# All of w_down in MLP groups 0 to 5 by seven products, with the 1/rms scale moved to the addition to the residual

## The chip, the cores and the metric

The kernel runs on one core of a Trainium2 chip. The metric is the device time of one execution in microseconds (us), the median of several runs. The engines are TensorE (PE in the profile, its weight loads PEld), VectorE (DVE), ScalarE (ACT), GpSimd (POOL) and SyncE (SP, which here only issues transfers).

## The reference

Two layers over 256 tokens of width 2048, all in float32. Each layer is a block of three attention groups and then an MLP; the change touches the MLP:

```python
h = rmsnorm(x, norm_mlp[l])
u = relu(h @ w_up[l])          # (256, 2048) @ (2048, 8192)
x = x + (u * u) @ w_down[l]    # (256, 8192) @ (8192, 2048)
```

`rmsnorm` multiplies a token's row by r = 1/sqrt(mean(x^2) + eps) and a column by its gain. Since r is positive and one number a token, relu(r a)^2 = r^2 relu(a)^2.

## The kernel before

Precision: a weight tile of float32 is split into a rounded part `hi` (format fp32r) and the rest `lo`; activations likewise. Three products (hi hi, lo hi, hi lo) stand for one float32 product. The split of a tile of 128 x 1024 (512 KB) is one cast on ACT (L1036) and one subtraction on DVE (L1037). `whi` and `wlo` have three buffers each, the raw tiles `wraw` five, `side` four, `spare0` and `spare1` one each.

The program is a list of `Step`s, one weight tile each. The main loop at the end of `tile_trunk` goes through it: it issues loads up to seven steps ahead on SP (`LOOK_LOAD`), splits two or three ahead, calls a step's `prep` five to eight ahead (`LOOK_PREP`, `LOOK_T2`, `LOOK_T3`), and then emits the step's matmuls. Tile's scheduler turns that into a fixed order for each engine, and may move an instruction past others that wait. `tick()` emits pieces of background work (the `add` queue) by their costs and due times.

The MLP is cut into eight groups `g` of 1024 columns of w_up, each of four blocks `q` of 256:

- `up_steps`: four steps a block, each with eight matmuls of 512 columns (L675: hi weights times hi and lo activations) and eight of 256 (L680: lo weights). At the fourth, `evac` copies the two banks out (L653 ACT, L654 DVE), takes the relu and multiplies by r (L655, one DVE instruction against `rrow`, r written along a row for all partitions), squares (ACT), splits into `u` (L660, L661), and `sums_of` makes the four sums S1 to S4 of the seven-product scheme from it (`sT`). `rrow` is built once a layer by `rows`: r on a diagonal, two fp32 matmuls with ones (L505), a copy.
- `strassen_steps(g, pair)`: Winograd's form of Strassen's scheme. A is u^2 of the group, its two token blocks times its blocks' two column halves; B is w_down, two halves along the sum times two blocks of 512 output columns. `pair` 0 is output columns 0 to 1023, `pair` 1 is 1024 to 2047. The sum of 1024 goes in two tiles, h = 0 and 1. The products in order are P1 = A11 B11, P2 = A12 B21, P7 = S3 (B12+B22), P6 = S2 (B22+B11+B12), P5 = S1 (B11+B12), P3 = S4 B22, P4 = A22 (B22+B11+B12+B21): each one step of six matmuls (L806) a tile. Bank `a` takes P1, P6, P5, P3, bank `d` takes P7 and P4; both lie in the one tile `S`. Bank `b` takes P2. After its product a bank is added to or subtracted from the residual `x` on DVE (L777) and, in `a` and `d`, accumulated on.
- Sums of weights come in two ways. `on_top` is a transfer from POOL that adds a tile from memory to one in SBUF (L792): on B11 for P2's step, on B12 for P7's, on P6's sum for P4. `sum_of` is a DVE addition (L788): P6's.
- `down_steps`: plain steps of twelve matmuls (L468, in `mode_b`), then an addition to `x` (L728).

In groups 0 to 5 the second half of the columns is mixed: its tile h = 0 goes by seven products (seven steps), its tile h = 1 plain, in four steps. Two of these (columns 1536 to 2047) have banks of their own; the two for columns 1024 to 1535 come at the end of the group and accumulate on banks `b` and `d` of the products. Groups 6 and 7 have seven products for the first half and plain steps for the second. While group g's down steps run, the up steps of group g + 1 are laid between them by a list `order` (1: a seven-product step, 0: another):

```python
for p_ in range(7):
    order += [1, 0, 1] + [0] * (p_ in (0, 1, 2, 4))
order += [0, 1] * 7 + [0, 0]
```

The rest of the MLP's frame: `hprep` transposes and splits the normalised input, `mlp_rs` computes r when the sums of squares are there, `layer_end` starts the next layer, `final_block` ends the program. The attention part has an addition to the residual with a scale per token already (L633, `scalar_tensor_tensor`).

Of the kernel before, what the change touches and what calls it, by code (L numbers as in the profile page):

```python
# [25 lines left out]
L = 2  # L26
# [17 lines left out]
def tile_trunk(ctx: ExitStack, tc: tile.TileContext, x_in, xt_in, w_in, w_o, w_up, w_down,  # L44
# [4 lines left out]
    D_X, D_S, D_SS, D_T, D_PV, D_QK, D_RQ, D_RK, D_SQ, D_R = 6.0, 6.0, 7.0, 18.0, 6.0, 6.0, 24.0, 16.0, 6.0, 4.0  # L49
# [52 lines left out]
    rrow = cp.tile([P, 256], F32, name="rrow")  # L102
# [350 lines left out]
    class Step:  # L453


        def __init__(self, src, kk, n, pre, mm, fourth=True, loads=None, prep=None, raw=None, post=None,
                     look=LOOK_PREP):
            self.look = look
            self.src, self.kk, self.n, self.pre, self.mm, self.fourth = src, kk, n, pre, mm, fourth
            self.loads, self.prep, self.raw, self.post = loads or [], prep, raw, post  # L460
# [27 lines left out]
    def layer_steps(l):  # L488
# [6 lines left out]
        def mlp_rs():  # L495
            r = rsqrt(mean_eps(st["ss2"], 4, 1.0 / D), 2)

            def rows():

                dg = mid(F32, 2, P)  # L500
                for t in range(NT):
                    nc.vector.tensor_scalar(dg[:, t, :], ident, r[:, t:t + 1], None, op0=ALU.mult)
                ps = tr_bank()
                for t in range(NT):
                    nc.tensor.matmul(ps[:, t * P:(t + 1) * P], full, dg[:, t, :], start=True, stop=True)  # L505
                nc.vector.tensor_copy(rrow, ps[:, 0:256])
                flags.add(("rrow", l))
            add(rows, 0.45, delay=D_R, front=True)
# [133 lines left out]
        def up_steps(g):  # L642

            out_, evacs = [], []
            for q in range(4 * g, 4 * g + 4):
                box = {}

                def evac(q=q, box=box):
                    need(("rrow", l))
                    a = mid(F32, 2, 256)  # L650
                    for i in range(2):

                        nc.scalar.copy(a[:, i, :], box["b"][i][:, 256:512])  # L653
                        nc.vector.tensor_add(a[:, i, :], a[:, i, :], box["b"][i][:, 0:256])  # L654
                    nc.vector.scalar_tensor_tensor(  # L655
                        a, a, 0.0, rrow.rearrange("p (o c) -> p o c", o=1).to_broadcast([P, 2, 256]),
                        op0=ALU.max, op1=ALU.mult)
                    nc.scalar.activation(a, a, AF.Square, bias=zero1[:, 0:1])
                    u = big(F32R, 2, 2, 256)
                    nc.scalar.copy(u[:, 0], a)  # L660
                    nc.vector.tensor_sub(u[:, 1], a, f(u[:, 0]))  # L661
                    uT[q] = u
                    sums_of(q, a)

                for s in range(4):
                    def pre(s=s):
                        need((("mlp", l), 2 * s + 1))

                    def mm(wh, wl, s=s, q=q, box=box, evac=evac):
                        if s == 0:  # L670
                            box["b"] = [mm_bank(), mm_bank()]
                        for kk in range(4):
                            ht = st["hT2"][2 * s + kk // 2][:, kk % 2, :]
                            for fs in range(2):
                                nc.tensor.matmul(box["b"][fs], wh[:, kk, fs * P:(fs + 1) * P], ht,  # L675
                                                 start=s == 0 and kk == 0, stop=False, skip_group_check=True)
                        for kk in range(4):
                            ht = st["hT2"][2 * s + kk // 2][:, kk % 2, :]
                            for fs in range(2):
                                nc.tensor.matmul(box["b"][fs][:, 0:256], wl[:, kk, fs * P:(fs + 1) * P], ht[:, 0:256],  # L680
                                                 start=False, stop=s == 3 and kk == 3, skip_group_check=True)
                        if s == 3 and q > 0:
                            evac()

                    out_.append(Step(w_up[l, q * 4 + s], 4, 256, pre, mm, fourth=False,
                                     post=evacs[0] if (q, s) == (1, 0) else None))
                    if s == 0:
                        evacs.append(evac)
            return out_
# [14 lines left out]
        def down_steps(gs, j, ks=range(4), shared=None):  # L704

            out_, box = [], {}
            tiles = [(g, k) for g in gs for k in ks]  # L710
            final = l == L - 1 and gs == (7,)
            for n, (g, k) in enumerate(tiles):
                def mm(wh, wl, g=g, k=k, n=n):
                    last = n == len(tiles) - 1
                    if n == 0:
                        box["b"] = [shared["b"], shared["d"]] if shared else [mm_bank(), mm_bank()]
                        box["w"] = []
                    hts = [uT[4 * g + k]] * 2
                    mode_b(box["b"], hts, wh, wl, [0, 1], n == 0 and not shared, last, blocks=(0,) if final else (0, 1),
# [6 lines left out]
                    def evac(t):  # L726
                        xs = x[:, t, j * 512:(j + 1) * 512]
                        nc.vector.tensor_add(xs, xs, box["b"][t])  # L728
                    if final:
# [4 lines left out]
                        for c in range(2):  # L734
# [5 lines left out]
                            with tc.issue_after(fin["base"]):  # L740
                                nc.vector.tensor_add(xs, xs, tail[c][:, 0:256])
# [10 lines left out]
                ti = (g * 4 + j) * 4 + k if g >= 6 else g * 16 + 12 + (j - 2) * 2 + k - 2  # L752
# [3 lines left out]
        def strassen_steps(g, pair=0, tiles=(0, 1), look=LOOK_T2):  # L756
# [7 lines left out]
            def src(par, j, h):  # L764
                return w_down[l, g * 16 + ((par * 2 + j) * 2 + h if pair == 0 else 8 + par * 2 + j)]
# [8 lines left out]
            def evac(bank, t, j, sign):  # L774
                xs = x[:, t, 1024 * pair + j * 512:1024 * pair + (j + 1) * 512]
                op = nc.vector.tensor_add if sign > 0 else nc.vector.tensor_sub
                op(xs, xs, bank)  # L777
# [16 lines left out]
            for name, lf, bk, fresh, dst in plan:  # L794
                for h in tiles:
                    def mm(wh, wl, name=name, lf=lf, bk=bk, fresh=fresh, dst=dst, h=h):
# [7 lines left out]
                        for a, w in ((0, wh), (1, wh), (0, wl)):  # L804
                            for i in range(2):
                                nc.tensor.matmul(o, ops[i][a], w[:, i, :], skip_group_check=True,  # L806
                                                 start=fresh and h == 0 and i == 0 and a == 0 and w is wh,
                                                 stop=h == tiles[-1] and i == 1 and w is wl)
                        if h == tiles[-1] and not (pair and name in ("P2", "P4")):
# [5 lines left out]
                    if name == "P1":  # L815
                        loads = [(("B11", h), src(0, 0, h), lambda h=h + pair: spare(F32, h))]
                        get = lambda h=h: raw["B11", h]
                    elif name == "P2":
                        loads = [(("B12", h), src(0, 1, h), None)]
# [4 lines left out]
                    elif name == "P7":  # L824
                        def prep(h=h):
                            on_top(raw["B12", h], 1, 1, h)
                        get = lambda h=h: raw["B12", h]
                    elif name == "P6":
                        loads = [(("B22", h), src(1, 1, h), None)]
# [15 lines left out]
                    def operand(get=get, key=(name, h)):  # L845
# [3 lines left out]
                               look={"P6": look, "P7": LOOK_T3}.get(name, LOOK_PREP),  # L849
# [3 lines left out]
            return out_, box  # L853

        steps.extend(up_steps(0))
        for g in range(8):

            if g < 6:
                up = up_steps(g + 1)
                ss = up[0:4] + down_steps((g,), 3, (2, 3)) + up[4:]  # L860
            elif g == 6:
                ss = up_steps(7)
            else:
                ss = down_steps((6, 7), 2) + down_steps((6,), 3) + down_steps((7,), 3)
            hs, _ = strassen_steps(g)
            if g < 6:
                more, shared = strassen_steps(g, 1, (0,), 4)
                hs += more

            if g < 6:  # L870
# [201 lines left out]
    for i, s in enumerate(steps):  # L1072
# [25 lines left out]
        if s.post:  # L1098
            s.post()
# [65 lines left out]
def _pack_down(w, g):  # L1165

    plain = [_pack(w[:, j * 512:(j + 1) * 512], 2) for j in range(4)]
    b = w.reshape(8, P, D)
    plain[0:2] = [np.stack([b[[4 * h + par, 4 * h + par + 2], :, j * 512:(j + 1) * 512].transpose(1, 0, 2).reshape(P, 1024)
                            for j in range(2) for h in range(2)]) for par in range(2)]  # L1170
    if g < 6:

        plain[2:4] = [np.stack([b[[par, par + 2], :, j * 512:(j + 1) * 512].transpose(1, 0, 2).reshape(P, 1024)
                                for par in range(2) for j in (2, 3)]), plain[2][2:4], plain[3][2:4]]
    return np.concatenate(plain)
# [60 lines left out]
```

## Time and profile before

| | |
|---|---|
| median of 3 runs | 1994.91 us (1994.78 to 1995.85) |
| the profiled execution | 1995.7 us, span 1993.9 us |
| mean granted TensorE clock | 0.999 |
| TensorE busy | 1980.3 us (99%), 10134 matmuls |
| DVE, ACT, POOL busy | 1647.0, 1247.4, 396.4 us |
| from HBM | 448.65 MB |

The span runs from the first to the last instruction of the profiled execution. In the rows of the profile, L and a number is a line of the kernel, `out<-in` are the program's names of tiles, `x` and a number is a count. In a row of windows stand the window's ends and length, then for PE, PEld, DVE, ACT and POOL the busy time with the instructions in brackets, then the granted clock, the busy share of the transfer engines and GB/s. In a row of the timeline stand the start, the time from the first start to the last end, the engine and the line. In a row of groups stand the count, the busy time in us and the mean of one in ns, and behind the last bar the engine's idle time ahead of them with what ended it. Matmuls are pipelined, so one lasts longer than the distance to the next.

### The profile page before, as it was taken

Reading aid. Unit: us, or ns where it says so; the run is one execution under the profiler, and the core shown is the slowest. Engines: PE = TensorE matmul, PEld = TensorE weight load, DVE = VectorE, ACT = ScalarE, POOL = GpSimd, SP = SyncE. Lnnn points to the kernel's source line nnn. Section 1 sums busy time; section 2 is a strip of 40 time slices with the busy share of each in tenths; the row PEclk is TensorE's granted clock in tenths of the full one; section 3 lists DMA queues with packets and bytes.
Section 4 is the critical chain, followed back from the end, with each engine's and each line's share of the span. In section 5 each row is a group of like instructions: output and inputs, shape, how many; then the busy total and the mean of one; then the engine's idle time right before and its main releaser. Section 6 shows DMA issues by size and latency. Waiting matters only on the chain.

```text
span 1993.9 us, 28351 instructions
## 1 busy us (share of the span) xinstructions
PE 1980.3 (99%) x10134; PEld 1683.2 (84%) x10134; DVE 1647.0 (83%) x2197; ACT 1247.4 (63%) x1778; POOL 396.4 (20%) x462
## 2 busy tenths in 40 slices
PE   9999999999999999999999999999999999999998
PEld 7888888888888888888888888888888888888887
DVE  6777877888888888888857678778988988888887
ACT  7667756666565656566656677566666656656664
POOL 0674620001010010100008745201010001101000
PEclk9999999999999999999999999999999999999999
DMA  9755755888888888978666467568898988989884
GB/s 341 212 164 153 235 168 190 224 260 260 252 256 243 273 248 251 273 224 252 207 190 201 153 177 222 169 190 251 233 273 243 269 248 247 265 252 260 238 264 126
DMA packets 128635, 456.31 MB, mean 229 GB/s; under 512 B 14660, under 2 KB 16964, under 8 KB 128493
## 3 DMA queue, kind: packets, MB, share of 16 engines
q1 hardware_dynamic: 109052, 384.18, 56.4%
q0 software_dynamic: 19008, 69.21, 20.1%
q8 instruction: 80, 1.31, 0.3%
q10 hardware_dynamic: 432, 1.10, 0.1%
q14 instruction: 63, 0.51, 0.1%
HBM read 448.65 MB, written 2.11 MB: 226 GB/s over the span
## 4 chain that ended last, share of the span: by engine, by line
PE 96%; DVE 1%; DMA 1%; ACT 1%; issue 1%; SPq 0%; POOL 0%; POOLq 0%; DVEq 0%; ACTq 0%
PE mm L468 32%; PE mm L675 23%; PE S L806 18%; PE mm L680 12%; PE mm L806 3%; PE S L468 2%; PE tr L380 1%; PE tr L399 1%; DMA wraw<-in_w_in_dram 1%; PE S L343 1%; PE S L342 1%; PE tr L223 1%; DVE wlo L1037 0%; ACT big L360 0%; PE tr L392 0%
## 5 line engine op out<-in xcount | busy, mean ns | idle before, releaser
L1037 DVE TENSOR_TENSOR wlo<-wraw,whi 128x1024 fp32r<-128x1024 f32 (+1 forms) x517 | 634.3, 1233 | 200.9 <-ACT whi L1036 191.4
L1036 ACT CAST whi<-wraw 128x1024 fp32r<-128x1024 f32 (+1 forms) x517 | 541.2, 1051 | 360.2 <-PE mm L675 100.2
L675 PE MATMUL mm<-big,whi 128*128 128x512 f32 x2048 | 514.1, 390 | 0.0
L468 PE MATMUL mm<-whi,big 128*128 128x512 f32 (+1 forms) x1692 | 500.1, 384 | 0.8 <-ACT whi L1036 0.8
L675 PEld LDWEIGHTS mm<-big,whi 128*128 128x128 f32 x2048 | 380.5, 188 | 79.4 <-ACT whi L1036 2.2
L468 PEld LDWEIGHTS mm<-whi,big 128*128 128x128 f32 x1692 | 314.3, 188 | 61.8 <-ACT whi L1036 1.9
L680 PEld LDWEIGHTS mm<-big,wlo 128*128 128x128 f32 x2048 | 280.9, 190 | 21.2
L468 PE MATMUL mm<-wlo,big 128*128 128x512 f32 (+1 forms) x846 | 293.3, 382 | 0.0
L806 PE MATMUL S<-whi,big 128*128 128x512 f32 x1056 | 290.1, 396 | 0.0
L680 PE MATMUL mm<-big,wlo 128*128 128x256 f32 x2048 | 287.3, 282 | 0.0
L806 PEld LDWEIGHTS S<-whi,big 128*128 128x128 f32 x1056 | 184.3, 189 | 34.2 <-DVE x L777 2.8
L468 PEld LDWEIGHTS mm<-wlo,big 128*128 128x128 f32 x846 | 159.3, 188 | 28.7
L806 PE MATMUL S<-wlo,big 128*128 128x512 f32 x528 | 163.4, 391 | 0.0
L1036 ACT CAST whi<-side 128x1024 fp32r<-128x1024 f32 x88 | 92.5, 1051 | 85.3 <-PE mm L675 76.6
L1036 ACT CAST whi<-big 128x1024 fp32r<-128x1024 f32 x88 | 92.9, 1056 | 77.5 <-DVE big L788 27.7
L468 PE MATMUL mm<-spare,big 128*128 128x512 f32 (+1 forms) x606 | 140.2, 380 | 0.0
L1037 DVE TENSOR_TENSOR wlo<-side,whi 128x1024 fp32r<-128x1024 f32 x88 | 107.7, 1224 | 35.4 <-ACT whi L1036 34.6
L792 POOL DMA_DIRECT2D spare<-in_w_down_dram x44 | 38.1, 866 | 476.2 <-DVE wlo L1037 458.4
L468 PEld LDWEIGHTS mm<-spare,big 128*128 128x128 f32 x606 | 108.9, 188 | 20.4
L1037 DVE TENSOR_TENSOR wlo<-big,whi 128x1024 fp32r<-128x1024 f32 x88 | 107.7, 1224 | 21.5 <-ACT whi L1036 21.3
L792 POOL DMA_DIRECT2D side<-in_w_down_dram x44 | 38.3, 881 | 400.9 <-DVE mid L654 150.8
L806 PEld LDWEIGHTS S<-wlo,big 128*128 128x128 f32 x528 | 99.2, 188 | 22.2
(163 smaller groups left out, 2310.3 us busy)
## 6 DMA issues: line engine op xcount, KB each, us to landing
wraw<-in_w_up_dram SPq DMA_DIRECT2D x256, 512.0 KB, 4.8
wraw<-in_w_down_dram SPq DMA_DIRECT2D x124, 512.0 KB, 5.1
wraw<-in_w_in_dram SPq DMA_DIRECT2D x119, 512.0 KB, 3.7
side<-in_w_down_dram SPq DMA_DIRECT2D x88, 512.0 KB, 5.2
wraw<-in_w_o_dram SPq DMA_DIRECT2D x64, 512.0 KB, 3.7
side<-in_w_down_dram POOLq DMA_DIRECT2D x44, 512.0 KB, 7.5
spare<-in_w_down_dram SPq DMA_DIRECT2D x44, 512.0 KB, 5.9
spare<-in_w_down_dram POOLq DMA_DIRECT2D x44, 512.0 KB, 5.5
```

The costliest lines, as they stand in the source:

```text
L223: nc.tensor.transpose(psv[:, kk, t, :], x[:, t, c0:c0 + P], ident)
L342: nc.tensor.matmul(o, st, u.kh[:, kh, :], start=True, stop=False)
L343: nc.tensor.matmul(o, st, u.kl[:, kh, :], start=False, stop=True)
L380: nc.tensor.transpose(ps[:, c * P:(c + 1) * P], u.p[:, s, kb * P:(kb + 1) * P], ident)
L399: nc.tensor.matmul(ps, u.V[:, kb, u.kv, :, :], pt[:, kb, :], start=n == 0, stop=n == 3)
L468: nc.tensor.matmul(banks[t][:, 0:n], a, (wl if part == "hl" else wh)[:, i, :], start=first and i == 0 and part == "hh", stop=last and i == ...
L675: nc.tensor.matmul(box["b"][fs], wh[:, kk, fs * P:(fs + 1) * P], ht, start=s == 0 and kk == 0, stop=False, skip_group_check=True)
L680: nc.tensor.matmul(box["b"][fs][:, 0:256], wl[:, kk, fs * P:(fs + 1) * P], ht[:, 0:256], start=False, stop=s == 3 and kk == 3, skip_group_ ...
L792: nc.gpsimd.dma_start(tile, src(par, j, h).rearrange("p (k n) -> p k n", k=2), accum_op=ALU.add)
L806: nc.tensor.matmul(o, ops[i][a], w[:, i, :], skip_group_check=True, start=fresh and h == 0 and i == 0 and a == 0 and w is wh, stop=h == ti ...
L1036: last_act[0] = nc.scalar.copy(h[:, part], w[:, part]).ins
L1037: last_lo[0] = nc.vector.tensor_sub(lo[:, part], w[:, part], f(h[:, part])).ins
```

## The change

In groups 0 to 5 the plain steps go, and both tiles of the second half go by seven products: 14 steps in place of 7 + 4. The packing of w_down (`_pack_down`) follows. Three of the four sums for P7 in a group (two halves, two tiles) are made by a transfer as before; the fourth (second half, h = 1) by `sum_of` on DVE, with B12 and B22 both loaded at P7's step.

The scale r moves: relu is now a plain relu on ACT, and each addition to the residual multiplies its bank by r^2 of its token (`scaled_add`, one `scalar_tensor_tensor`, with -r^2 for a subtraction). `rows` and `rrow` go; r^2 and -r^2 are two small instructions on POOL in `mlp_rs`. The first block's `evac` no longer waits for `rrow` and stands at its own fourth step. `order` is rewritten: 44 steps a group in place of 41, with up steps between the seven-product steps and two of these in a row at every other place.

```diff
         def mlp_rs():
-            r = rsqrt(mean_eps(st["ss2"], 4, 1.0 / D), 2)
-
-            def rows():
...
-            add(rows, 0.45, delay=D_R, front=True)
+            nc.gpsimd.tensor_tensor(r2[:, l, 0], mean_eps(st["ss2"], 4, 1.0 / D), mone[:, 0:NT], op=ALU.pow)
+            nc.gpsimd.tensor_scalar(r2[:, l, 1], r2[:, l, 0], -1.0, None, op0=ALU.mult)
...
                 def evac(q=q, box=box):
-                    need(("rrow", l))
...
-                    nc.vector.scalar_tensor_tensor(
-                        a, a, 0.0, rrow.rearrange("p (o c) -> p o c", o=1).to_broadcast([P, 2, 256]),
-                        op0=ALU.max, op1=ALU.mult)
+                    nc.scalar.activation(a, a, AF.Relu, bias=zero1[:, 0:1])
                     nc.scalar.activation(a, a, AF.Square, bias=zero1[:, 0:1])
...
+        def scaled_add(xs, bank, t, sign=1):
+            col = r2[:, l, (1 - sign) // 2, t:t + 1]
+            nc.vector.scalar_tensor_tensor(xs, bank, col, xs, op0=ALU.mult, op1=ALU.add)
...
             def evac(bank, t, j, sign):
-                xs = x[:, t, 1024 * pair + j * 512:1024 * pair + (j + 1) * 512]
-                op = nc.vector.tensor_add if sign > 0 else nc.vector.tensor_sub
-                op(xs, xs, bank)
+                scaled_add(x[:, t, 1024 * pair + j * 512:1024 * pair + (j + 1) * 512], bank, t, sign)
...
                     elif name == "P7":
+                        if h not in moved:
+                            loads = [(("B12", h), src(0, 1, h), None), (("B22", h), src(1, 1, h), None)]
+
                         def prep(h=h):
-                            on_top(raw["B12", h], 1, 1, h)
+                            if h in moved:
+                                on_top(raw["B12", h], 1, 1, h)
+                            else:
+                                sum_of(raw["B12", h], raw["B12", h], raw["B22", h])
...
-                               look={"P6": look, "P7": LOOK_T3}.get(name, LOOK_PREP),
+                               look={"P6": LOOK_T2, "P7": LOOK_T3 if h in moved else LOOK_PREP}.get(name, LOOK_PREP),
...
             if g < 6:
-                more, shared = strassen_steps(g, 1, (0,), 4)
-                hs += more
-
-            if g < 6:
+                hs += strassen_steps(g, 1, (0,))
                 order = []
-                for p_ in range(7):
-                    order += [1, 0, 1] + [0] * (p_ in (0, 1, 2, 4))
-                order += [0, 1] * 7 + [0, 0]
-                ss += down_steps((g,), 2, (2, 3), shared)
+                for p_ in range(14):
+                    order += [1, 0, 1] if p_ < 13 else [1, 1]
+                    order += [0] * (p_ in (0, 4, 8))
```

More of the change, by code (lines that the diff above doesn't have):

```diff
@@ L101, in tile_trunk @@
     nc.vector.memset(full, 1.0)
-    rrow = cp.tile([P, 256], F32, name="rrow")
+    r2 = cp.tile([P, L, 2, NT], F32, name="r2")
     mhalf = cp.tile([P, 16], F32, name="mhalf")
@@ L453, in tile_trunk, with __init__ @@
     class Step:
[L456 removed]
+        def __init__(self, src, kk, n, pre, mm, fourth=True, loads=None, prep=None, raw=None,
                      look=LOOK_PREP):
@@ L681, in mm @@
                                                  start=False, stop=s == 3 and kk == 3, skip_group_check=True)
-                        if s == 3 and q > 0:
+                        if s == 3:
                             evac()
[L685 to L688, printed above, removed]
+                    out_.append(Step(w_up[l, q * 4 + s], 4, 256, pre, mm, fourth=False))
             return out_
@@ L715, in mm @@
                     if n == 0:
-                        box["b"] = [shared["b"], shared["d"]] if shared else [mm_bank(), mm_bank()]
+                        box["b"] = [mm_bank(), mm_bank()]
                         box["w"] = []
                     hts = [uT[4 * g + k]] * 2
-                    mode_b(box["b"], hts, wh, wl, [0, 1], n == 0 and not shared, last, blocks=(0,) if final else (0, 1),
+                    mode_b(box["b"], hts, wh, wl, [0, 1], n == 0, last, blocks=(0,) if final else (0, 1),
                            lo_last=gs != (7,))
@@ L794, in strassen_steps @@
             for name, lf, bk, fresh, dst in plan:
-                for h in tiles:
+                for h in range(2):
                     def mm(wh, wl, name=name, lf=lf, bk=bk, fresh=fresh, dst=dst, h=h):
@@ L807, in mm @@
                                                  start=fresh and h == 0 and i == 0 and a == 0 and w is wh,
-                                                 stop=h == tiles[-1] and i == 1 and w is wl)
-                        if h == tiles[-1] and not (pair and name in ("P2", "P4")):
+                                                 stop=h == 1 and i == 1 and w is wl)
+                        if h == 1:
                             evac(o, *dst)
@@ L815, in strassen_steps @@
                     if name == "P1":
-                        loads = [(("B11", h), src(0, 0, h), lambda h=h + pair: spare(F32, h))]
+                        loads = [(("B11", h), src(0, 0, h), lambda h=h: spare(F32, h))]
                         get = lambda h=h: raw["B11", h]
                     elif name == "P2":
-                        loads = [(("B12", h), src(0, 1, h), None)]
+                        loads = [(("B12", h), src(0, 1, h), None)] if h in moved else []
                         def prep(h=h):
@@ L1165, in _pack_down, with by_parity @@
 def _pack_down(w, g):
-    plain = [_pack(w[:, j * 512:(j + 1) * 512], 2) for j in range(4)]
     b = w.reshape(8, P, D)
[L1169 to L1175, printed above, removed]
+    def by_parity(c):
+        return [np.stack([b[[4 * h + par, 4 * h + par + 2], :, j * 512:(j + 1) * 512].transpose(1, 0, 2).reshape(P, 1024)
+                          for j in (c, c + 1) for h in range(2)]) for par in range(2)]
+    right = by_parity(2) if g < 6 else [_pack(w[:, j * 512:(j + 1) * 512], 2) for j in (2, 3)]
+    return np.concatenate(by_parity(0) + right)
 def _pack_inputs(inp):
```

46 lines of the change are left out of this document (15 added, 31 removed).

## The prediction

> **What bounds the kernel now.** I read the page's busy times first, then its chain, then windows cut at the repeating unit of the long middle part (one group of the MLP), then the matmuls of one group in order of time.
>
> ```profile
> span 1993.9 us, 28351 instructions
> PE 1980.3 (99%) x10134; PEld 1683.2 (84%) x10134; DVE 1647.0 (83%) x2197; ACT 1247.4 (63%) x1778; POOL 396.4 (20%) x462
> PE 96%; DVE 1%; DMA 1%; ACT 1%; issue 1%; SPq 0%; POOL 0%; POOLq 0%; DVEq 0%; ACTq 0%
> ...
> 458.20:542.90 84.70, 84.70 (x433) 71.88 (x432) 74.44 (x93) 51.73 (x61) 7.77 (x9) 1.00 0.86 254
> 542.90:627.50 84.60, 84.60 (x433) 71.85 (x432) 74.44 (x93) 51.76 (x61) 7.76 (x9) 1.00 0.87 255
> ```
>
> A group takes 84.65 us (the two windows have the same counts on every engine, so they are one period). In it DVE works 74.4 us (88%), ACT 51.7, POOL 7.8, and the transfer engines are busy 0.86 to 0.87 of the time. TensorE never stops in these rows, but ends of matmuls are modelled, so I check by starts.
>
> ```profile
> 504.81 1.98 PE L675 MATMUL mm<-big,whi 128*128 128x512 f32 x8
> 506.62 1.12 PE L680 MATMUL mm<-big,wlo 128*128 128x256 f32 x8
> 507.57 1.09 PE L806 MATMUL S<-whi,big 128*128 128x512 f32 x4
> 508.50 0.62 PE L806 MATMUL S<-wlo,big 128*128 128x512 f32 x2
> 508.96 1.98 PE L675 MATMUL mm<-big,whi 128*128 128x512 f32 x8
> ...
> 549.25 1.98 PE L468 MATMUL mm<-whi,big 128*128 128x512 f32 x8
> 551.07 1.07 PE L468 MATMUL mm<-wlo,big 128*128 128x512 f32 x4
> 551.97 1.07 PE L806 MATMUL S<-whi,big 128*128 128x512 f32 x4
> ```
>
> The first column is the start. An up step costs 507.57 - 504.81 = 2.76 us, one step of a seven-product scheme (six matmuls) 508.96 - 507.57 = 1.39, a plain down step (twelve) 551.97 - 549.25 = 2.72. A group holds 16, 21 and 4 of them: 44.16 + 29.19 + 10.88 = 84.23, of the 84.65 measured. So 0.42 us a group is all that TensorE waits: it is the bound, and its work is what the change has to shorten.
>
> **The change, part by part.**
>
> *Matmuls.* In a group 0 to 5, columns 1024 to 2047 cost 7 x 1.39 + 4 x 2.72 = 20.61 us now and 14 x 1.39 = 19.46 after: 1.15 less. (Six matmuls fewer at 0.227 would be 1.36; steps of six are dearer per matmul, 1.39/6 = 0.232, so I take the steps.) Two layers of six groups: **-13.8 us**, all on the path.
>
> *The row of 1/rms.* Once a layer `rows` disappears with its fp32 matmuls.
>
> ```profile
> 325.00 0.60 PE L505 MATMUL tr<-mid,full 128*128 128x128 f32 x4
> 325.37 2.09 PE L675 MATMUL mm<-big,whi 128*128 128x512 f32 x8
> ```
>
> 325.37 - 325.00 = 0.37, twice: **-0.7 us**. In its place stand two small POOL instructions a layer, needed only at the first addition to the residual, a whole group later: nothing.
>
> *VectorE and ScalarE.*
>
> ```profile
> L1037 DVE TENSOR_TENSOR wlo<-wraw,whi 128x1024 fp32r<-128x1024 f32 x515 | 633.0, 1235 | 200.9 <-ACT whi L1036 191.4 <-issue 7.9 <-PE tr L223 0.4
> L1036 ACT CAST whi<-wraw 128x1024 fp32r<-128x1024 f32 x515 | 540.0, 1052 | 360.2 <-PE mm L675 100.2 <-PE S L806 96.4 <-PE mm L468 75.0
> L777 DVE TENSOR_TENSOR x<-x,S 128x512 f32<-128x512 f32 x156 | 106.5, 683 | 1.3 <-PE S L806 1.1
> L788 DVE TENSOR_TENSOR big<-side,spare 128x1024 f32<-128x1024 f32 x44 | 53.6, 1219 | 0.0
> L654 DVE TENSOR_TENSOR mid<-mid,mm 128x256 f32<-128x256 f32 x128 | 47.8, 415 | 0.7
> L658 ACT ACTIVATE mid<-mid,zero 128x512 f32<-128x512 f32 x64 | 46.2, 722 | 15.2 <-DVE mid L655 15.2
> L655 DVE SCALAR_TENSOR_TENSOR mid<-mid,rrow 128x512 f32<-128x512 f32 x64 | 44.0, 687 | 0.7
> L661 DVE TENSOR_TENSOR big<-mid,big 128x512 fp32r<-128x512 f32 x64 | 43.8, 685 | 0.0
> L633 DVE SCALAR_TENSOR_TENSOR x<-mm,sm,x 128x512 f32<-128x512 f32 x48 | 33.9, 744 | 0.2
> ```
>
> Per group DVE gains three splits (44 steps for 41: 3 x 1.235 = 3.7) and two weight sums (the sixth and the untransferred seventh of the second half: 2 x 1.219 = 2.4); it loses four relu-and-scale (4 x 0.687 = 2.7) and two of sixteen additions to the residual (1.4); the other fourteen become scaled. The nearest row for that is L633, the same form in the attention part: 0.744 for 0.683, 14 x 0.06 = 0.9. Balance +2.9: 77.3 of 83.5 us, 93% for 88. ACT gains four relu (nearest row L658, 0.72) and three casts: +6.0, 69%. On the mean both stay under TensorE, so their cover is its matmuls; what that cover lacks in places is the next term and the second rival. The relu follows the additions of L654 on ACT, ahead of the square, and delays `u` by about as much as L655 did; `u` is used a group later.
>
> *Waits for the accumulator.* The pair of banks `S` is freed only when the last addition has read it. Before, the only such seams in a group are the plain steps' end before the next P1, and P6 before P5.
>
> ```profile
> 531.00 1.75 PE L675 MATMUL mm<-big,whi 128*128 128x512 f32 x7
> 532.70 1.21 PE L806 MATMUL S<-whi,big 128*128 128x512 f32 x4
> 533.75 0.62 PE L806 MATMUL S<-wlo,big 128*128 128x512 f32 x2
> ...
> 478.73 0.51 PE L680 MATMUL mm<-big,wlo 128*128 128x256 f32 x3
> 479.07 1.16 PE L806 MATMUL S<-whi,big 128*128 128x512 f32 x4
> 480.07 0.62 PE L806 MATMUL S<-wlo,big 128*128 128x512 f32 x2
> ...
> PEld S L806 <- DVE x L777: 2.8, 15, 0.3
> PEld S L806 <- DVE x L728: 2.7, 10, 0.4
> ```
>
> At both the scheduler has pulled matmuls of the following up step ahead of the waiting product (seven at 531.00, written after P1 in the program), so the addition's 0.68 us is mostly covered. What is left: seven at 0.227 end at 532.59, P1 starts at 532.70, and its four take 1.05 for 0.93: 0.23 us. At 479.07 four take 1.00: 0.07. The last two lines, from the waits (total, times, longest), say that no single wait went over 0.4. After the change the list has no up step between P4 and P1 of the second half, none between its P6 and P5, none between its P5 and P3. The old seam at the group's end stays (P4 in place of the plain steps). New: one like P1's and two like P5's, 0.23 + 2 x 0.07 = 0.37. Bounds: nothing (the scheduler may fill them whole; below nothing is excluded, since a wait can't be negative and the old seam remains), or a whole addition uncovered at each of three, 3 x 0.744 = 2.2. I take 0.37, since both seams above are filled in this way: 12 x 0.37 = **+4.4 us**.
>
> *Transfers and queues.*
>
> ```profile
> q1 hardware_dynamic: 109052, 384.18, 56.4%
> q0 software_dynamic: 19008, 69.21, 20.1%
> spare<-in_w_down_dram POOLq DMA_DIRECT2D x44, 512.0 KB, 5.5
> side<-in_w_down_dram POOLq DMA_DIRECT2D x44, 512.0 KB, 7.5
> ```
>
> SP issues 32 weight loads a group before and after (three `wraw` fewer, two `side` and one `spare` more): nothing. POOL issues eleven adding transfers for nine; POOL itself is 91% idle. On the transfer engines one costs 20.1% x 1993.9 / 132 = 3.04 us (three kinds of 44, two shown), so 73.2 becomes 79.3 of 83.5: 95%. A transfer that lands later delays the DVE sum queued for it and every split behind that sum. In the first half P1 to P6 shrinks by two up steps (5.5 us). I cost it at nothing: by the loads' own rows, landing takes 5.5 to 7.5 us, and between P2's transfer and P6's sum there are still four steps of 84.65 / 41 = 2.06 each. The cover is thin: if all of a landing's spread (2 us) showed once a group it would be +24.
>
> **Sum.** -13.8 - 0.7 + 4.4 = -10.1. The profiled execution took 1995.7 (span 1993.9 and 1.8 around it), 0.8 above the median of 1994.91; taken from the median that gives **1984.8 us**, span about 1983.8.
>
> **The rivals.**
>
> *Full gain.* The scheduler fills the new seams as well: 1994.9 - 14.5 = 1980.4. For it: pulled matmuls at every seam. Against: none of them was filled to zero.
>
> *The seam at the end of a group (slower).* The list ends with four seven-product steps in a row (P3, P4, P4, then the next P1), right behind the up step that closes a block of `u`. DVE then owes 4 x 1.235 of splits, 2 x 0.744 of additions, and at least 2 x 0.415 + 2 x 0.685 of `u`'s work (L654, L661 and the like split of the sums): 8.6 us, while TensorE has 4 x 1.39 = 5.6, plus the 1.39 of one step split ahead. Uncovered, 1.6 us a group is +19.7 over twelve: 1994.9 - 14.5 + 4.4 + 19.7 = 2004.5. It turns the change into a loss from 10.1/12 = 0.84 us a group. For it: DVE's slack shrinks from 10.2 to 6.2 us a group, and the plain steps that gave slack here (2.72 us for one split) are gone. Against: `u`'s work isn't urgent, and up steps on both sides give the time back within 15 us.
>
> *Transfers become the bound (slower).* It needs the two added transfers to cost 84.65 - 73.2 = 11.4 us of engine time, 5.7 each for 3.04; at 7.5 each, the longer landing, a group takes 88.2, +43: 2038. Milder, a spread of 2 us at one sum a group: 2009. For it: 95%. Against: no DVE sum waited at all (L788, idle 0.0). [...]
>
> *Nothing changes.* TensorE's load port is busy 71.88 of 84.70 (85%), so TensorE may have 15% of room and the group's time be set elsewhere: 1994.9. Against: starts of matmuls are 0.227 apart throughout, without gaps. [...] The spacing decides here, I think.
>
> **How the numbers follow.** Forecast 0.40 (its own range 1981.5 to 1989); full gain 0.22; group's end 0.22, of which a third stays faster, a third is about even and a third slower; transfers 0.10; nothing 0.06. Within 0.2% (4 us) a measurement of this kernel can't tell from no change. Faster: 0.40 + 0.22 + 0.08 = 0.70; same 0.06 + 0.07 = 0.13; slower 0.10 + 0.07 = 0.17. The range runs from just below full gain, 1979.5, to 1999: it leaves out the worse half of the group's end, most of the transfers' case and little else, below 2 in 10.
>
> **What would show it.** Right: 72 matmuls fewer, and L505's 8; a group's period of 83.3 to 83.9; steps of 1.39 and 2.76 unchanged; short waits of L806 on the scaled additions (up to five a group, 0.1 to 0.4 each); DVE about 93%. Wrong: gaps of a microsecond ahead of P1 with DVE full (group's end); L788's line or ACT's casts waiting on transfers; scaled additions well off 0.744; a table load on ACT among the relus.

## The result, and the profile after

The changed kernel takes 2049.91 us (median of 5 runs, 2047.15 to 2057.72) against 1995.23 for the kernel before: the ratio is 1.0283 [1.0269, 1.0296], slower. The forecast was 1984.8, and the range ended at 1999. Single runs of four of the kernels below took 1.4 to 2.4 times as long as their other runs, and are in no median here.

In the changed file the products are L787, the up steps L662 and L667, a split's cast L1015 (ACT) and subtraction L1016 (DVE), the adding transfers L773 (`on_top`), the scaled addition L689, and L642 to L645 are `evac` (L643 the addition on DVE that completes the copy of a bank, L644 the relu). The experiments' files differ by a few lines: a split is L1016 and L1017 in the first, L1017 and L1018 in the third, L1018 and L1019 with both repairs, and the products are L789 where bank `d` has a tile of its own. The page after, its span and busy times, then its chain by engine and the landing of the adding transfers for P4:

```profile
span 2054.7 us, 28448 instructions
PE 1988.0 (97%) x10054; PEld 1681.3 (82%) x10054; DVE 1675.0 (82%) x2163; ACT 1325.6 (65%) x1878; POOL 419.4 (20%) x488
PE 83%; DMA 10%; ACT 3%; DVE 2%; issue 1%; POOL 0%; SPq 0%; POOLq 0%; ACTq 0%; DVEq 0%
big<-in_w_down_dram POOLq DMA_DIRECT2D x56, 512.0 KB, 10.1
```

The 80 matmuls are gone (10134 to 10054), and yet TensorE's busy time rose from 1980.3 to 1988.0, and its idle time from 13.6 to 66.7 us. Transfers, 1% of the chain before, are now 10%. Windows cut at the repeating unit (ends, length, PE, PEld, DVE, ACT and POOL, granted clock, transfer engines' share, GB/s):

```profile
622.10:708.60 86.50, 83.42 (x424) 70.47 (x424) 77.15 (x91) 56.54 (x68) 9.53 (x11) 1.00 0.89 257
708.60:799.10 90.50, 86.25 (x424) 72.55 (x424) 77.41 (x91) 57.45 (x68) 9.53 (x11) 0.96 0.88 250
799.10:889.20 90.10, 85.00 (x424) 71.61 (x424) 77.43 (x91) 57.59 (x69) 9.55 (x11) 0.98 0.86 252
```

A group takes 86.5 to 90.5 us, not 83.3 to 83.9. DVE and ACT are as busy as forecast (77.4 and 57.5 us a group), and TensorE has lost 3 to 5 us a group to something else, plus some of its clock. It is one gap a group. The waits of the whole program (engine, line, what ended it: total, times, longest) have ten of the twelve in the first line; in group 5 of each layer the gap stands at an up step instead, behind a late cast (second line). The third line is ACT's wait for the transfers:

```profile
PE S L787 <- ACT mid L644: 46.0, 10, 7.4
PE mm L662 <- ACT whi L1015: 7.2, 2, 4.6
ACT whi L1015 <- DMA big<-in_w_down_dram: 32.9, 9, 6.0
```

The windows around one gap show what it costs (behind the window's length stand PE and PEld):

```profile
708.60:712.70 4.10, 0.00 (x0) 0.00 (x0) 2.65 (x5) 3.26 (x5) 0.00 (x0) 0.92 1.02 420
712.70:718.30 5.60, 5.55 (x13) 4.43 (x14) 3.83 (x7) 3.29 (x4) 0.86 (x1) 0.50 0.59 110
```

For 4.1 us no matmul runs; for the 5.6 us after it the granted clock is 0.50, and 13 matmuls stand where 24 would. The chain of work through the gap (start, length, what):

```profile
695.10 13.78 DMA big<-in_w_down_dram
708.98 1.05 ACT whi L1015
710.05 0.58 DVE wlo L1016
711.20 0.76 DVE mid L643 x2
711.98 0.73 ACT mid L644
712.75 5.46 PE S L787 x12
```

It begins with a transfer that takes 13.78 us: the one that adds B21 to P6's sum in the second tile, for P4. POOL's part of the timeline points at the reason (start, length, engine, line, in brackets the idle time before it and what ended it), first after, then before:

```profile
690.71 0.86 POOL L773 DMA_DIRECT2D side<-in_w_down_dram  x1 [13.60 <-DVE wlo L1016]
691.24 1.22 POOL L773 DMA_DIRECT2D big<-in_w_down_dram  x1
693.22 0.86 POOL L773 DMA_DIRECT2D side<-in_w_down_dram  x1 [0.76 <-DMA side<-in_w_down_dram]
695.10 0.86 POOL L773 DMA_DIRECT2D big<-in_w_down_dram  x1 [1.01 <-DVE wlo L1016]
```

```profile
469.18 0.86 POOL L792 DMA_DIRECT2D big<-in_w_down_dram  x1 [2.61 <-DVE wlo L1037]
476.39 0.86 POOL L792 DMA_DIRECT2D big<-in_w_down_dram  x1 [6.35 <-DVE wlo L1037]
489.32 0.86 POOL L792 DMA_DIRECT2D side<-in_w_down_dram  x1 [12.06 <-DMA wraw<-in_w_up_dram]
492.62 0.86 POOL L792 DMA_DIRECT2D side<-in_w_down_dram  x1 [2.44 <-DVE x L777]
...
511.20 0.86 POOL L792 DMA_DIRECT2D big<-in_w_down_dram  x1 [12.21 <-PE mm L675]
```

After, at the end of this group, POOL issues four adding transfers of 512 KB within 4.4 us (4.1 to 9.9 at the ends of the six groups of this layer). The two `side` are the seventh sums of the next group's first half (P7), used in the group that has not begun; the two `big` are what P4 waits for now. They land in the order of issue, 7.1, 10.0, 11.8 and 13.8 us behind their issues, which is 3.4 to 3.9 us apart. The program calls the `prep` of these two P7 sums only at the first steps of the next group, behind that of both `big`, so the scheduler has moved them forward; that it did so because their operands were there and POOL was free is a reading of the listing. Before, too, the next group's two P7 transfers (489.32 and 492.62) went ahead of the last one for P4 (511.20), but 18.6 us ahead of it, and the other neighbours in these rows lie 3 to 13 us apart.

The rest is order within an engine. DVE around the gap, and the products:

```profile
710.05 1.22 DVE L1016 TENSOR_TENSOR wlo<-big,whi 128x1024 fp32r<-128x1024 f32 x1 [2.70 <-ACT whi L1015]
711.20 0.74 DVE L643 TENSOR_TENSOR mid<-mid,mm 128x256 f32<-128x256 f32 x2
711.86 0.74 DVE L689 SCALAR_TENSOR_TENSOR x<-S,r,x 128x512 f32<-128x512 f32 x1
707.86 0.62 PE L787 MATMUL S<-wlo,big 128*128 128x512 f32 x2
712.75 2.05 PE L787 MATMUL S<-whi,big 128*128 128x512 f32 x4 [4.27 <-ACT mid L644]
```

P3's product ends at 708.48. Its addition L689 stands in DVE's order behind the split of P4's *second* tile and the additions of `evac` (L643), so it runs at 711.86, 3.4 us late, and ends at 712.60. P4's *first* tile, whose split was through by 707.36, starts at 712.75, 0.15 after that addition. P3 uses bank `a` and P4 bank `d`, but both are in the one tile `S`, so P4 waits for the addition from `a`. The profile puts the wait down to the relu L644, which ended at 712.70; that P4 has no use for `mid`, and which of the two it was, the third experiment tells.

### The profile page after: what moved, and what is told of

Same layout as the page of the kernel before. It is cut to its first block, busy times and chain, and to the rows that moved or that the text cites. A ratio compares the mean times of both kernels' runs of the same rounds, so it can differ in the third digit from the quotient of the medians.

```text
span 2054.7 us, 28448 instructions
## 1 busy us (share of the span) xinstructions
PE 1988.0 (97%) x10054; PEld 1681.3 (82%) x10054; DVE 1675.0 (82%) x2163; ACT 1325.6 (65%) x1878; POOL 419.4 (20%) x488
## 4 chain that ended last, share of the span: by engine, by line
PE 83%; DMA 10%; ACT 3%; DVE 2%; issue 1%; POOL 0%; SPq 0%; POOLq 0%; ACTq 0%; DVEq 0%
PE mm L468 25%; PE mm L662 20%; PE S L787 19%; PE mm L667 10%; DMA big<-in_w_down_dram 6%; PE mm L787 4%; DMA side<-in_w_down_dram 2%; ACT whi L1015 1%; DMA wraw<-in_w_in_dram 1%; PE tr L380 1%; PE tr L399 1%; DVE wlo L1016 1%; PE S L343 1%; ACT mid L644 1%; PE S L342 1%
## 5 line engine op out<-in xcount | busy, mean ns | idle before, releaser
L1016 DVE TENSOR_TENSOR wlo<-wraw,whi 128x1024 fp32r<-128x1024 f32 (+1 forms) x481 | 590.5, 1234 | 184.8 <-ACT whi L1015 175.5
L1015 ACT CAST whi<-wraw 128x1024 fp32r<-128x1024 f32 (+1 forms) x481 | 501.5, 1048 | 321.3 <-PE mm L662 118.1
L662 PE MATMUL mm<-big,whi 128*128 128x512 f32 x2048 | 512.0, 391 | 7.2 <-ACT whi L1015 7.2
L662 PEld LDWEIGHTS mm<-big,whi 128*128 128x128 f32 x2048 | 383.9, 189 | 87.7 <-ACT whi L1015 8.1
L787 PE MATMUL S<-whi,big 128*128 128x512 f32 x1344 | 384.2, 408 | 46.1 <-ACT mid L644 46.0
L468 PE MATMUL mm<-whi,big 128*128 128x512 f32 (+1 forms) x1404 | 423.4, 384 | 0.5 <-ACT whi L1015 0.5
L787 PEld LDWEIGHTS S<-whi,big 128*128 128x128 f32 x1344 | 245.0, 196 | 100.7 <-ACT mid L644 50.0
L468 PEld LDWEIGHTS mm<-whi,big 128*128 128x128 f32 x1404 | 260.1, 188 | 49.9 <-ACT whi L1015 1.4
L667 PEld LDWEIGHTS mm<-big,wlo 128*128 128x128 f32 x2048 | 280.9, 190 | 21.2
L667 PE MATMUL mm<-big,wlo 128*128 128x256 f32 x2048 | 287.3, 282 | 0.0
L468 PE MATMUL mm<-wlo,big 128*128 128x512 f32 (+1 forms) x702 | 253.0, 381 | 0.0
L787 PE MATMUL S<-wlo,big 128*128 128x512 f32 x672 | 214.4, 401 | 0.0
L773 POOL DMA_DIRECT2D spare<-in_w_down_dram x56 | 48.5, 865 | 738.8 <-DVE wlo L1016 703.7
L1016 DVE TENSOR_TENSOR wlo<-big,whi 128x1024 fp32r<-128x1024 f32 x112 | 136.7, 1221 | 64.1 <-ACT whi L1015 64.1
L1015 ACT CAST whi<-side 128x1024 fp32r<-128x1024 f32 x112 | 118.0, 1053 | 105.8 <-PE mm L662 65.3
L1015 ACT CAST whi<-big 128x1024 fp32r<-128x1024 f32 x112 | 117.9, 1053 | 92.6 <-PE S L787 51.6
L1015 ACT CAST whi<-spare 128x1024 fp32r<-128x1024 f32 x112 | 117.5, 1049 | 62.5 <-PE S L787 34.4
L1016 DVE TENSOR_TENSOR wlo<-side,whi 128x1024 fp32r<-128x1024 f32 x112 | 136.6, 1220 | 24.7 <-ACT whi L1015 16.1
L787 PEld LDWEIGHTS S<-wlo,big 128*128 128x128 f32 x672 | 130.2, 194 | 29.9
L1016 DVE TENSOR_TENSOR wlo<-spare,whi 128x1024 fp32r<-128x1024 f32 x112 | 136.7, 1220 | 10.3 <-ACT whi L1015 6.5
## 6 DMA issues: line engine op xcount, KB each, us to landing
big<-in_w_down_dram POOLq DMA_DIRECT2D x56, 512.0 KB, 10.1
```

Of the source, the lines that this page charges most:

```text
L468: nc.tensor.matmul(banks[t][:, 0:n], a, (wl if part == "hl" else wh)[:, i, :], start=first and i == 0 and part == "hh", stop=last and i == ...
L773: nc.gpsimd.dma_start(tile, src(par, j, h).rearrange("p (k n) -> p k n", k=2), accum_op=ALU.add)
L1015: last_act[0] = nc.scalar.copy(h[:, part], w[:, part]).ins
L1016: last_lo[0] = nc.vector.tensor_sub(lo[:, part], w[:, part], f(h[:, part])).ins
```

## The experiments

Ratios are against the kernel before, with 95% intervals. Edits are to the changed kernel unless the text says otherwise.

**POOL's order alone.** The P7 transfers of a half (column block of 1024) are issued behind the last transfer for P4 of the half before.

```diff
-    last_lo, last_act, last_load = [None], [None], [None]
+    last_lo, last_act, last_load, last_top = [None], [None], [None], [None]
...
-                                on_top(raw["B12", h], 1, 1, h)
+                                with tc.issue_after(last_top[0]) if last_top[0] is not None else nullcontext():
+                                    on_top(raw["B12", h], 1, 1, h)
...
-                            on_top(t2[h], 1, 0, h)
+                            last_top[0] = on_top(t2[h], 1, 0, h)
```

> All of the change, with one edge more: each transfer that makes a seventh sum is issued on POOL behind the last transfer that adds to P6's sum (for P4) of the half before; no work is changed. Theory 1 (late transfer: at each group's end the next group's two seventh-sum transfers get ahead of, or between, the two transfers that P4 waits for, so that the last lands 3 to 7 us late): the twelve gaps of 2.8 to 7.5 us go, the time falls by 55 to 70 us to 1980 to 1992 us. Theory 2 (four seven-product steps in a row: VectorE and ScalarE owe too much there, the transfer is incidental): VectorE's and ScalarE's work is the same, so 2040 to 2055. Theory 3 (P4 waits for P3's addition, since both banks are in one tile, and the addition is queued on VectorE behind the split that waits for the transfer): as theory 1, with up to 0.5 us a group left, 1985 to 1995.

Measured: 1997.00 us, ratio 1.0007 [0.9998, 1.0016], 2 us above the third theory's range and 5 above the first's, far from the second's. Some 53 us come back by the order of transfers alone, with the same transfers, bytes and arithmetic. POOL at a group's end, the median landing of `big` (10.1 before this edit), and what is left of the gap:

```profile
594.98 0.86 POOL L773 DMA_DIRECT2D big<-in_w_down_dram  x1 [13.72 <-DVE wlo L1017]
599.25 0.86 POOL L773 DMA_DIRECT2D big<-in_w_down_dram  x1 [3.40 <-DVE wlo L1017]
599.79 2.11 POOL L773 DMA_DIRECT2D side<-in_w_down_dram  x2
...
big<-in_w_down_dram POOLq DMA_DIRECT2D x56, 512.0 KB, 7.1
...
612.01 0.62 PE L787 MATMUL S<-wlo,big 128*128 128x512 f32 x2
612.56 0.74 DVE L643 TENSOR_TENSOR mid<-mid,mm 128x256 f32<-128x256 f32 x2
613.22 0.74 DVE L689 SCALAR_TENSOR_TENSOR x<-S,r,x 128x512 f32<-128x512 f32 x1
614.11 1.16 PE L787 MATMUL S<-whi,big 128*128 128x512 f32 x4 [1.48 <-ACT mid L644]
...
PE S L787 <- ACT mid L644: 15.1, 10, 1.8
```

Both splits of P4 are done in time here, and TensorE still stops once a group: P3's addition stands behind `evac`'s two additions L643, and P4 behind P3's addition. The start of P4 is 614.11 - 612.01 = 2.10 after that of P3's last two matmuls, which need 2 x 0.227: 1.65 us of nothing, ten times by the last line.

**The seventh sums of the first half by DVE** in groups 0 to 5: at a group's end no P7 transfer can get ahead of P4's.

```diff
-            hs = strassen_steps(g)
+            hs = strassen_steps(g, 0, () if g < 6 else (0, 1))
```

> All of the change, but in groups 0 to 5 the first half's two seventh sums are made by additions on VectorE in place of transfers (one of four by transfer, where the change has three). Theory 1: without the two transfers that get in the way P4's come in time, the gaps go; VectorE has 2.4 us a group more (about 79.8 of 83.4), so 1983 to 2000. Theory 2: VectorE owes more, so no gain: 2045 to 2080.

Measured: 2011.47 us, ratio 1.0088 [1.0072, 1.0103], between the two ranges expected. Better than the change by 38 us, worse than the first experiment by 14. Its waits (engine, line, what ended it: total, times, longest):

```profile
PE S L787 <- ACT mid L644: 15.1, 10, 1.8
PE mm L662 <- ACT whi L1015: 7.4, 4, 3.7
PEld mm L667 <- DVE wlo L1016: 6.5, 12, 1.3
```

The first line is that of the first experiment to the tenth, so the large gaps were the transfers' doing and the 1.65 us are not. The other two are new or larger waits for splits: DVE now makes these sums, and that this is what makes the splits late is the likely reading, not a measured one. The transfers are worth keeping.

**A bank of its own for P4 (and P7)**, transfers left as they were:

```diff
+                        if (name, h) == ("P7", 0) and g < 6:
+                            box["d"] = mm_bank()
```

> All of the change, but bank d of groups 0 to 5 (P7, P4) is a tile of its own from the other six banks, so P4 no longer shares a tile with the bank whose addition follows P3. Theory 3: P4's first tile runs while the transfer for the second is awaited, and the wait behind VectorE's queue goes: 2.5 to 4 us a group less, 2000 to 2020. Theory 1: P4's second tile still waits for the landing; only the 1.4 us of the first tile and the additions' delay are won, 2015 to 2038. Theory 2: 2045 to 2055.

Measured: 2004.86 us, ratio 1.0041 [1.0028, 1.0055]. Its waits:

```profile
ACT whi L1017 <- DMA big<-in_w_down_dram: 34.2, 10, 4.8
PE mm L789 <- ACT whi L1017: 11.9, 9, 2.3
...
697.08 1.07 PE L789 MATMUL mm<-whi,big 128*128 128x512 f32 x4
700.84 1.21 PE L789 MATMUL mm<-whi,big 128*128 128x512 f32 x4 [2.24 <-ACT whi L1017]
702.62 0.74 DVE L689 SCALAR_TENSOR_TENSOR x<-S,r,x 128x512 f32<-128x512 f32 x1
```

ACT still waits 34.2 us for late transfers (32.9 in the changed kernel), but the wait behind L644 is gone. P4's first tile (697.08, in its own bank `mm`) runs 5.5 us ahead of P3's addition (702.62), and only the second (700.84) is late. So it was the shared tile and P3's addition that held P4, and the relu that the profile named was only the event that came last.

**The scale part alone**: the kernel *before* with r^2 at the additions and a plain relu on ACT, groups' steps and order as they were.

```diff
-            r = rsqrt(mean_eps(st["ss2"], 4, 1.0 / D), 2)
...
+            nc.gpsimd.tensor_tensor(r2[:, l, 0], mean_eps(st["ss2"], 4, 1.0 / D), mone[:, 0:NT], op=ALU.pow)
...
-                    nc.vector.scalar_tensor_tensor(
-                        a, a, 0.0, rrow.rearrange("p (o c) -> p o c", o=1).to_broadcast([P, 2, 256]),
-                        op0=ALU.max, op1=ALU.mult)
+                    nc.scalar.activation(a, a, AF.Relu, bias=zero1[:, 0:1])
...
-                        nc.vector.tensor_add(xs, xs, box["b"][t])
+                        scaled_add(x[:, t, j * 512:(j + 1) * 512], box["b"][t], t)
```

> The kernel before with the scale's part alone: r squared at the additions to the residual, relu on ScalarE, no row of r; the products and their order as before. If the scaled additions and the relu cost nothing on the path (prediction): the two fp32 matmuls of the row go, 1993.5 to 1995.2. If the longer chain for u or the longer additions (0.06 us each) are a cause of the loss: over 2000, by 0.5 us a group or more.

Measured: 1991.80 us, ratio 0.9981 [0.9972, 0.9990]: 3.8 us less, 1.7 below the range expected without a cost. This half of the change is harmless and a little better than costed.

**Both repairs**: the first and the third experiment together.

> Both repairs at once: the seventh sums' transfers are issued behind the transfers for P4 of the half before, and bank d is a tile of its own. Theory A (the loss is two waits: a late transfer, and P4 behind P3's addition through the shared tile): both go, and the time is the prediction's 1.15 us a group less work and no row of r, with the small seams of P6, P5 and P1 left: 1981 to 1986 us. Theory B (VectorE at 93%, four seven-product steps in a row, sets the pace at a group's end whatever the waits): 1990 to 1997, near the 1997.0 of the run with the order alone.

Measured: 1976.40 us, ratio 0.9907 [0.9890, 0.9923], 19.3 us below the kernel before and 4.6 below the range of theory A. A group (the next one has the same length), and the page's busy times:

```profile
458.20:541.50 83.30, 83.30 (x429) 71.06 (x428) 76.72 (x93) 57.42 (x69) 9.60 (x11) 1.00 0.92 271
...
PE 1963.3 (99%) x10054; PEld 1670.3 (85%) x10054; DVE 1663.4 (84%) x2163; ACT 1323.4 (67%) x1878; POOL 420.5 (21%) x488
```

The period is 83.30 and TensorE doesn't stop. In its span of 1976.0 it is idle for 12.7 us, against 66.7 in the changed kernel, and busy for 24.7 us less with the same 10054 matmuls. The two sum to 78.7, the whole difference of the profiled spans (the profiled execution of the changed kernel was 6.5 us above its median). Order alone gave 53 us, the bank alone 45, both 73.5, so they overlap by 24. Part of that is the clock: its mean is 0.986 in the changed kernel and 0.999 and 0.998 in the two, and TensorE's busy time falls by 20.8 us with the order, 15.3 with the bank and 24.7 with both, so that 11 count twice. The rest is idle time, 37.8, 35.3 and 54.0 less: in one and the same gap TensorE waits for both things, and either repair shortens it.

**Another filling for the same place**: the order list ends with an up step between P4's two tiles, taken from the group's start, where one up step fewer stands behind P1. Transfers and banks are left as in the change.

```diff
-                    order += [1, 0, 1] if p_ < 13 else [1, 1]
-                    order += [0] * (p_ in (0, 4, 8))
+                    order += [1, 0, 1]
+                    order += [0] * (p_ in (4, 8))
```

> All of the change, with the list of steps alone altered: one up step stands between P4's two tiles at the end of the group, taken from the group's start (extra up steps after places 4 and 8 in place of 0, 4 and 8). Theory A: the up step fills the wait behind P3's addition (1.6 us) and gives the late transfer 2.8 us more, so 2.8 to 4.4 us a group: 1997 to 2016. Theory B (the four steps in a row are the cause by themselves): the whole loss goes, 1980 to 1992.

Measured: 1996.20 us, ratio 0.9998 [0.9989, 1.0008], just below the range of theory A. Its waits:

```profile
ACT whi L1015 <- DMA big<-in_w_down_dram: 26.0, 7, 4.5
PE S L787 <- DVE x L689: 6.2, 8, 0.9
```

The transfers for P4 still come late (their median landing is 11.7 us, 10.1 in the changed kernel; ACT's wait is 26.0 us, 32.9 there), and 54 us of the loss are gone: an up step's matmuls of 2.76 us lie where the gap was. What a late transfer costs here depends on the work that lies beside it.

**All four seventh sums by transfers**, on top of both repairs: the transfer engines get one more adding transfer a group, DVE one sum less.

```diff
-                hs += strassen_steps(g, 1, (0,))
+                hs += strassen_steps(g, 1)
```

> As the run with both repairs, and the last of the four seventh sums too by a transfer: one VectorE addition of 1.22 us less and one transfer of 3.04 us of engine time more a group. If neither engine bounds (A): within 3 us of the run with both repairs. If VectorE's load still costs: 3 to 12 us faster than it. If the transfer engines, at about 98% then, are the bound: 10 us slower or more.

Measured: 1975.28 us, ratio 0.9901 [0.9885, 0.9918], not told apart from both repairs alone. Two groups in one window:

```profile
458.20:625.00 166.80, 166.80 (x854) 141.96 (x853) 152.43 (x182) 115.24 (x138) 20.98 (x24) 1.00 0.96 280
```

At a share of 0.96 and 280 GB/s (the changed kernel: 0.86 to 0.89 and 250 to 257) TensorE doesn't wait. Bandwidth is not what the change ran out of.

**Both repairs and the other order**, and then that with the four transfers too, **everything together**:

> As the run with both repairs, and the up step at the end of the group as well. A: only the last seam (P4 before the next P1) could gain, and the group's start loses an up step: within 3 us of the run with both repairs. B: 5 us or more faster than it.

> Both repairs, all four seventh sums by transfers, and the up step at the end of the group. The two last runs each took the waits of the MLP of a layer to about half a microsecond, so there is nothing left for both together: A (TensorE's work is the bound) says within 1.5 us of either, 1974 to 1976.5. If the transfers, now 98% on paper and with an up step fewer at the group's start, begin to bound: over 1978.

Measured: 1975.08 us, ratio 0.9899 [0.9882, 0.9915], and 1975.18, ratio 0.9896 [0.9880, 0.9913], both as expected. Once both waits are gone nothing is left there for a third measure. These two and the four transfers are all 1.0% below the kernel before, and the intervals don't tell them apart.

## Why the prediction was wrong, step by step

- *Matmuls, -13.8*: right. Both repairs against the scale part alone differ by 0.0074 in the ratio, 14.8 us (with intervals of 0.0009 and 0.0017 some 4 us either way): this is the part of seven products for plain steps once its two waits are gone. The steps now sum to 16 x 2.76 + 28 x 1.39 = 83.08 us of the period of 83.30.
- *The row of 1/rms, -0.7*: the whole scale part came to -3.8 [-5.6, -2.0]. The term itself is not refuted, but something of 3 us more wasn't in it. It is hardly in the gaps: in the profile of the scale part alone TensorE is idle for 13.1 us, 13.6 before, and busy for 3.5 less; the up steps' 2048 matmuls of hi weights alone take 4.7 less (514.1 us before, 509.4 there). What shortens them isn't settled.
- *VectorE and ScalarE, hidden*: right in size (77.4 us a group for 77.3, 57.5 of ACT for 69% of 83.5), and in the forms (ACT's relu, L644, took 0.724 for 0.722):

```profile
L689 DVE SCALAR_TENSOR_TENSOR x<-S,r,x 128x512 f32<-128x512 f32 x168 | 125.5, 747 | 7.1 <-PE S L787 6.6
```

  That is 0.747 us for the 0.744 forecast. Both repairs run at this load without a stop: it was the order on DVE, not its sum, that cost.
- *Transfers and queues, nothing*: **this step failed**, and the larger part of the loss is here: 53 us by the order alone, 28.5 where bank `d` has its own tile already. It read a mean (POOL 91% idle) and medians of landing (5.5 to 7.5 us), and asked how many transfers there are, not which goes ahead of which. With two transfers for P4 at the group's end where there had been one, the next group's P7 sums were issued among them; the last of the four landed late. Its warning ("if all of a landing's spread (2 us) showed once a group it would be +24") had the right form; its size is near the 28.5 and less than half of the 53, which is luck either way: the last transfer landed 13.78 us after its issue, 6.7 more than the median of 7.1 in the first experiment, not 2 more. It was placed on DVE's weight sum (L788), while the wait came in ACT's cast for P4, as one of the signs of a wrong forecast said ("ACT's casts waiting on transfers").
- *Waits for the accumulator, +4.4*: **this failed too**. The step named three new seams (P4 to P1, P6 to P5, P5 to P3) and not P3 to P4, which uses another bank, although the step itself says that the *pair* `S` is freed by the last addition. In the first half P3 and P4 stand next to each other in both lists, with an up step behind P4's first tile for the scheduler to pull ahead, and no wait of this kind goes over 0.5 us there; at the end of the new list no up step is left. The price is 1.65 us in a group with late transfers repaired, 20.6 in all by the first experiment against both repairs. It lies in the bounds of 0 to 2.2 a group only by luck, since these were meant for three other seams. For those the +4.4 was too much: with both repairs 83.30 - 83.08 = 0.22 us a group is left for every wait, 0.42 before.
- The rival at the group's end had place and price (1.6 us a group, +19.7) by another mechanism, too much work on DVE. Both repairs refute that, since DVE has the same work there, so the agreement in size is chance. The rival in which transfers become the bound had the engine right and the reason wrong: the transfers were late by their order, and the share of 0.96 costs nothing in the run with four transfers (1975.28 us, 1976.40 with both repairs).
- Not in the prediction at all: the drop of the granted clock behind gaps, to 0.50 for the 5.6 us behind the one above.

So the sum is: -19.3 by what the change does when it runs freely (more than even the full gain of -14.5, by the scale part above all), and +73.5 by these two waits and the clock.

## What to carry to other kernels

A queue that is mostly idle is not harmless: ask which transfers may now be issued ahead of the one that is needed next, since a mean share and a median landing of the kernel before (here POOL 91% idle, 5.5 to 7.5 us) don't show it, and tie the early ones behind the urgent one. When a list of steps is rewritten, go through *every* pair of neighbours that share a tile, not only a bank, and look at what stands in the engine's order between the first's end and the instruction that frees it (here a split and two additions, and P3's addition ran 3.4 us late). Where the last steps of a list have no independent work behind them, look there for late items: here TensorE stopped once a group, for 4.1 us in the gap shown and for 1.65 with the transfers in order.

## What was not expected of the hardware

Some gaps cost more than their length. In the 5.6 us behind the gap of 4.1 above, 13 matmuls are 0.43 us each in place of 0.227, with the clock at 0.50; the gaps of 1.65 us in the first experiment left the mean clock at 0.999. Length alone doesn't decide in between. Two stretches of the changed kernel, the first behind a gap of 3.15 us, the second behind one of 2.65:

```profile
625.05 1.17 PE L787 MATMUL S<-whi,big 128*128 128x512 f32 x4 [3.15 <-ACT mid L644]
...
626.51 1.09 PE L787 MATMUL S<-whi,big 128*128 128x512 f32 x4
...
444.62 1.17 PE L787 MATMUL S<-whi,big 128*128 128x512 f32 x4 [2.65 <-ACT mid L644]
445.62 0.91 PE L787 MATMUL S<-wlo,big 128*128 128x512 f32 x2
446.33 1.91 PE L787 MATMUL S<-whi,big 128*128 128x512 f32 x4
```

The longer gap leaves full speed: the granted clock is 1.00 from 625.05 to 631.00. Behind the shorter one the third row, 1.7 us after the restart, is at half speed: the clock is 0.50 from 446.33 to 448.89, and four matmuls last 1.91 us together, 1.09 behind the longer gap. What decides between these two gaps no run here shows.
